# Rotary embedding on one core: whole-row stores and loads replaced by alternating two-position pieces

## The chip, the cores and the metric

The kernel runs on one core of one Trainium2 chip. The metric is the device time of one execution in microseconds (us), as the median of several runs. The core has its compute engines (TensorE, VectorE, ScalarE, GpSimd; DVE in the profile is VectorE, ACT is ScalarE, POOL is GpSimd), SyncE (SP), which issues transfers, and 16 DMA engines that move all data between main memory (HBM) and the on-chip memory (SBUF, 128 partitions).

## What is computed

The reference rotates pairs of neighbouring elements by an angle that depends on the position in the sequence. The sizes are 8 batch rows, 2048 positions, 16 heads, 64 elements per head; everything is fp32.

```python
x1 = x_pairs[..., 0]
x2 = x_pairs[..., 1]
out1 = x1 * cos - x2 * sin
out2 = x1 * sin + x2 * cos
out = np.stack([out1, out2], axis=-1).reshape(batch, seq_len, num_heads, head_dim)
```

The input and the output have 67.1 MB each, so the kernel reads and writes 134 MB of main memory; the tables have 0.26 MB each.

## The kernel before

**Tiling.** The 2048 positions of a batch row are split into 128 partitions of 16 consecutive positions (`K = 16`). In main memory the 16 positions of one partition lie together, 64 KB of fp32. On the chip a batch row is one tile of bf16, `[128, 16, 1024]`, 32 KB per partition. Loads turn fp32 into bf16 and stores turn bf16 into fp32 on the way; both are DMAs issued by GpSimd, on one queue (q0 in the profile), which the DMA engines work off in order.

**Compute.** VectorE rotates four positions at a time (`KP = 4`) with three instructions: the tile times the sine table into `qt` (line 74), the tile times the cosine table in place (line 75), and the sum of the tile and `qt` with the two elements of each pair swapped (line 80). Before that it builds the bf16 tables: `s_tab` with alternating signs (lines 94 and 95) and `c_tab` with each value twice (line 96).

**Order of the work.** The order on each engine is the order of the program text (`manual_schedule`); only the waits are placed by the framework. SP loads the first two positions of batch row 0 in fp32 (`head`, line 85, two DMAs), then the cosine table (line 86) and the sine table (line 87). GpSimd issues the load of the rest of row 0 and of rows 1 to 4, so five tiles are asked for at once (`NX = 5`, line 56). ScalarE turns the head into bf16 (line 92). Then, for each batch row, VectorE rotates it, GpSimd stores the whole row (line 59), and from the second row on GpSimd loads a further row into the tile that the row before has left; that load waits until the store of that earlier row has landed. So rows 5, 6 and 7 are loaded between the stores.

**The tail.** Of the last row GpSimd stores twelve positions. The last four (`TAIL = 4`) are turned to fp32 by ScalarE (line 117) into the buffer that the head had used and stored by SP (line 118). A one-element ScalarE copy (line 116) ahead of it writes into the tile of row 6, so it waits for that row's store.

A DMA of 128 partitions is spread over the 16 DMA engines, eight partitions to each; the trace's packet records show one packet for each partition and contiguous run.

Of the kernel before, what the change touches and what calls it, by code (L numbers as in the profile page):

```python
# [2 lines left out]

# [4 lines left out]


@with_exitstack  # L10
def kernel(
    ctx: ExitStack,
    tc: tile.TileContext,
    x: bass.AP,
    cos: bass.AP,
    sin: bass.AP,
    out: bass.AP,
):
    nc = tc.nc
    fp32 = mybir.dt.float32  # L20
    bf16 = mybir.dt.bfloat16
    mult = mybir.AluOpType.mult
    add = mybir.AluOpType.add

    B, S, H, D = x.shape
    P = 128
    K = S // P
    KP = 4
    D2 = D // 2
    HD = H * D  # L30
    NX = 5
    HEAD = 2
    TAIL = 4


    x_t = x.rearrange("b (p k) h d -> b p k (h d)", p=P, k=K)
    out_t = out.rearrange("b (p k) h d -> b p k (h d)", p=P, k=K)
    cos_t = cos.rearrange("(p k) c -> p (k c)", p=P, k=K)
    sin_t = sin.rearrange("(p k) c -> p (k c)", p=P, k=K)

    consts = ctx.enter_context(tc.tile_pool(name="consts", bufs=1))
    xpool = ctx.enter_context(tc.tile_pool(name="xpool", bufs=NX))
    qpool = ctx.enter_context(tc.tile_pool(name="qpool", bufs=1))
    stage = ctx.enter_context(tc.tile_pool(name="stage", bufs=1))

    cos_sb = consts.tile([P, K * D2], fp32)
    sin_sb = consts.tile([P, K * D2], fp32)
    c_tab = consts.tile([P, K, D], bf16)
    s_tab = consts.tile([P, K, D], bf16)

    tiles = {}

    def load(b, k0=0):
        if b not in tiles:
            tiles[b] = xpool.tile([P, K, HD], bf16, name="xt")
        nc.gpsimd.dma_start(out=tiles[b][:, k0:], in_=x_t[b, :, k0:])  # L56

    def store(b, k1=K):
        nc.gpsimd.dma_start(out=out_t[b, :, :k1], in_=tiles[b][:, :k1])  # L59

    def rotate(b, k0, k1):
        nk = k1 - k0
        xp = tiles[b][:, k0:k1]
        qt = qpool.tile([P, KP, HD], bf16, name="qt")

        def rows(a):
            return a.rearrange("p k (h e) -> p k h e", h=H, e=D)

        def tab(a):
            return dataclasses.replace(  # L70
                a, offset=a.offset + k0 * D, ap=[a.ap[0], [D, nk], [0, H], [1, D]]
            )

        nc.vector.tensor_tensor(out=rows(qt[:, :nk]), in0=rows(xp), in1=tab(s_tab), op=mult)  # L74
        nc.vector.tensor_tensor(out=rows(xp), in0=rows(xp), in1=tab(c_tab), op=mult)  # L75
        q_swap = dataclasses.replace(
            qt, offset=qt.offset + 1, ap=[qt.ap[0], [2, nk * HD // 2], [-1, 2]]
        )
        x3 = xp.rearrange("p k (a j) -> p (k a) j", j=2)
        nc.vector.tensor_tensor(out=x3, in0=x3, in1=q_swap, op=add)  # L80

    with tc.manual_schedule():
        head = stage.tile([P, TAIL, HD], fp32, name="st")
        for k in range(HEAD):
            nc.sync.dma_start(out=head[:, k : k + 1], in_=x_t[0, :, k : k + 1])  # L85
        nc.sync.dma_start(out=cos_sb, in_=cos_t)
        nc.sync.dma_start(out=sin_sb, in_=sin_t)
        load(0, HEAD)
        for b in range(1, NX):
            load(b)  # L90

        nc.scalar.copy(out=tiles[0][:, :HEAD], in_=head[:, :HEAD])  # L92
        s2 = s_tab.rearrange("p k (i j) -> p (k i) j", j=2)
        nc.vector.tensor_copy(out=s2[:, :, 0], in_=sin_sb)  # L94
        nc.vector.tensor_scalar_mul(s2[:, :, 1], sin_sb, -1.0)  # L95
        nc.vector.tensor_copy(  # L96
            out=c_tab.rearrange("p k (i j) -> p (k i) j", j=2),
            in_=cos_sb.to_broadcast([P, K * D2, 2]),
        )
        for b in range(B):  # L100
            if b == 0:
                rotate(b, 0, HEAD)
                rotate(b, HEAD, KP)
            for k0 in range(KP if b == 0 else 0, K, KP):
                rotate(b, k0, k0 + KP)
            if b < B - 1:
                store(b)

            if b >= 1 and b - 1 + NX < B:
                load(b - 1 + NX)  # L110
        store(B - 1, K - TAIL)

        tail = stage.tile([P, TAIL, HD], fp32, name="st")
        nc.scalar.copy(out=tiles[B - 2][:1, 0, :1], in_=tiles[B - 1][:1, K - 1, :1])  # L116
        nc.scalar.copy(out=tail, in_=tiles[B - 1][:, K - TAIL :])  # L117
        nc.sync.dma_start(out=out_t[B - 1, :, K - TAIL :], in_=tail)


# [1 line left out]
_INS = ['x', 'cos', 'sin']  # L122
_OUTS = [((8, 2048, 16, 64), 'float32')]


# [23 lines left out]
```

## Time and profile before

| | |
|---|---|
| median of 3 runs | 317.44 us (317.4 to 317.5) |
| span of the profiled execution | 316.0 us |
| VectorE busy | 221.8 us, 102 instructions |
| ScalarE busy | 6.9 us |
| GpSimd busy | 8.9 us |
| one VectorE instruction on four positions | 2.29 us |
| issue of one DMA on GpSimd | 0.53 to 0.67 us |
| first VectorE instruction, start of the last | at 44.2 us, at 267.1 us |

The span is the time from the first to the last instruction in one execution that the hardware profiler recorded. The page divides it into 40 equal slices; a digit is the busy share of that slice in tenths. The row named DMA is the mean share of the 16 DMA engines, and the row GB/s is what they moved, counted at the destination: a load counts with its bf16 bytes and a store with its fp32 bytes. The part on queues gives for each the packets, the megabytes and the share of the engines' time. The waits name an engine and a line, what it waited for, and then the microseconds in total, how often, and the longest.

### The profile page before, as it was taken

How to read it: one execution, taken by the hardware profiler on the slowest of the kernel's cores; microseconds unless marked ns; L12 is line 12 of the kernel's file. 1: busy time of each engine (PE TensorE's matmuls, PEld its weight loads, DVE VectorE, ACT ScalarE, POOL GpSimd, SP SyncE). 2: the span in 40 equal slices, each digit the busy share in tenths (PEclk: the TensorE clock that was granted, in tenths of full speed). 3: DMA queues.
4: the chain of work that ended last, by engine and by line, in shares of the span. 5: the costliest groups of instructions: out<-in, count | busy, mean ns of one | idle time of the engine just before them, and what ended most of it. 6: DMA issues, size and time to landing. Idle time of an engine off the chain costs nothing.

```text
span 316.0 us, 198 instructions
## 1 busy us (share of the span) xinstructions
DVE 221.8 (70%) x102; ACT 6.9 (2%) x4; POOL 8.9 (3%) x20
## 2 busy tenths in 40 slices
DVE  0000039999999999999999999999999999100000
ACT  1200000000000000000000000000000000000400
POOL 3000000000000000000000000000000000000000
DMA  9899999999999999999999999999999999999996
GB/s 241 198 257 212 212 207 236 228 199 199 253 212 265 398 498 431 398 332 261 203 399 465 328 203 199 481 448 265 199 307 423 398 440 481 406 398 481 417 431 263
DMA packets 3025, 101.72 MB, mean 322 GB/s; under 512 B 336, under 2 KB 336, under 8 KB 848
## 3 DMA queue, kind: packets, MB, share of 16 engines
q0 software_dynamic: 2304, 98.04, 96.8%
q1 hardware_dynamic: 720, 3.67, 3.1%
q14 instruction: 1, 0.01, 0.0%
HBM read 67.63 MB, written 67.11 MB: 426 GB/s over the span
## 4 chain that ended last, share of the span: by engine, by line
another core or an unknown queue 91%; DMA 2%; ACTq 1%; ACT 1%; SPq 0%; issue 0%
DMA st<-in_x_dram 2%; ACTq L144 1%; ACT xt L92 1%; ACT L92 0%; SPq L85 0%; ACT xt L116 0%; ACTq L116 0%; ACTq L92 0%
## 5 line engine op out<-in xcount | busy, mean ns | idle before, releaser
L75 DVE TENSOR_TENSOR xt<-xt,c_tab 128x4096 bf16<-128x4096 bf16 (+1 forms) x33 | 73.5, 2228 | 1.1
L80 DVE TENSOR_TENSOR xt<-xt,qt 128x4096 bf16<-128x4096 bf16 (+1 forms) x33 | 73.5, 2228 | 1.1
L74 DVE TENSOR_TENSOR qt<-xt,s_tab 128x4096 bf16<-128x4096 bf16 (+1 forms) x33 | 73.5, 2228 | 1.1
L94 DVE CAST s_tab<-sin_sb 128x512 bf16<-128x512 f32 x1 | 0.5, 453 | 44.2 <-DMA sin_sb<-in_sin_dram 44.2
L59 POOL DMA_DIRECT2D out_dram<-xt x8 | 4.3, 535 | 202.1 <-DVE xt L80 202.1
L116 ACT COPY xt<-xt 1x1 bf16<-1x1 bf16 x1 | 0.2, 193 | 286.3 <-DMA out_dram<-xt 286.3
L56 POOL DMA_DIRECT2D xt<-in_x_dram x8 | 4.4, 561 | 52.1 <-DMA out_dram<-xt 51.3
L117 ACT CAST st<-xt 128x4096 f32<-128x4096 bf16 x1 | 3.6, 3599 | 0.0
L92 ACT CAST xt<-st 128x2048 bf16<-128x2048 f32 x1 | 1.9, 1899 | 0.0
L92 ACT ACT_TABLE_LOAD x1 | 1.3, 1283 | 6.4 <-DMA st<-in_x_dram 6.4
L96 DVE CAST c_tab<-cos_sb 128x1024 bf16<-128x1024 f32 x1 | 0.7, 684 | 0.0
L95 DVE TENSOR_SCALAR s_tab<-sin_sb 128x512 bf16<-128x512 f32 x1 | 0.4, 443 | 0.0
L133 POOL MEMSET const-float32-0.0<- 128x1 f32 x1 | 0.1, 99 | 0.2 <-issue 0.2
L133 POOL MEMSET const-bfloat16-1.0<- 128x1 bf16 x1 | 0.1, 102 | 0.0
L133 POOL MEMSET const-float32-1.0<- 128x1 f32 x1 | 0.1, 99 | 0.0
L133 POOL MEMSET const-uint8-127<- 128x1 uint8 x1 | 0.1, 99 | 0.0
## 6 DMA issues: line engine op xcount, KB each, us to landing
xt<-in_x_dram POOLq DMA_DIRECT2D x7, 4096.0 KB, 58.0
out_dram<-xt POOLq DMA_DIRECT2D x1, 6144.0 KB, 49.4
xt<-in_x_dram POOLq DMA_DIRECT2D x1, 3584.0 KB, 22.7
out_dram<-st SPq DMA_DIRECT2D x1, 2048.0 KB, 15.5
st<-in_x_dram SPq DMA_DIRECT2D x2, 512.0 KB, 4.5
cos_sb<-in_cos_dram SPq DMA_DIRECT2D x1, 256.0 KB, 22.4
sin_sb<-in_sin_dram SPq DMA_DIRECT2D x1, 256.0 KB, 42.1
out_dram<-xt POOLq DMA_DIRECT2D x7, 54.0
```

The source lines that it names most:

```text
L56: nc.gpsimd.dma_start(out=tiles[b][:, k0:], in_=x_t[b, :, k0:])
L59: nc.gpsimd.dma_start(out=out_t[b, :, :k1], in_=tiles[b][:, :k1])
L74: nc.vector.tensor_tensor(out=rows(qt[:, :nk]), in0=rows(xp), in1=tab(s_tab), op=mult)
L75: nc.vector.tensor_tensor(out=rows(xp), in0=rows(xp), in1=tab(c_tab), op=mult)
L80: nc.vector.tensor_tensor(out=x3, in0=x3, in1=q_swap, op=add)
L92: nc.scalar.copy(out=tiles[0][:, :HEAD], in_=head[:, :HEAD])
L94: nc.vector.tensor_copy(out=s2[:, :, 0], in_=sin_sb)
L95: nc.vector.tensor_scalar_mul(s2[:, :, 1], sin_sb, -1.0)
L96: nc.vector.tensor_copy(out=c_tab.rearrange("p k (i j) -> p (k i) j", j=2), in_=cos_sb.to_broadcast([P, K * D2, 2]),)
L117: nc.scalar.copy(out=tail, in_=tiles[B - 1][:, K - TAIL :])
L133: nc = _bacc.Bacc("TRN2", target_bir_lowering=False, num_devices=1)
L144: with _tile.TileContext(nc) as tc:
```

## The change

From batch row 2 on, loads come in pieces of two positions (`CH = 2`, 8 KB of fp32 per partition). After each of rows 0 to 5 is rotated, GpSimd issues eight pairs in turn: the store of two positions of row b and the load of the same two positions of row b + 2 (`LEAD = 2`). Rows 0 and 1 are loaded as before, and rows 6 and 7 are each stored by one DMA; the fp32 tail with its ScalarE copies and its SP store is gone. There are four fixed tiles instead of a pool of five, and row b uses tile b mod 4. SP loads the sine table first, then the cosine table, then the head in one DMA. The VectorE instructions and their order are the same.

```diff
-    NX = 5
+    NX = 4
+    LEAD = 2
     HEAD = 2
-    TAIL = 4
+    CH = 2
...
+    head = consts.tile([P, HEAD, HD], fp32)
+    qt = consts.tile([P, KP, HD], bf16)
+    xb = [consts.tile([P, K, HD], bf16, name=f"xt{i}") for i in range(NX)]
...
+    def load(b, k0, k1):
+        nc.gpsimd.dma_start(out=xb[b % NX][:, k0:k1], in_=x_t[b, :, k0:k1])
...
+    def store(b, k0, k1):
+        nc.gpsimd.dma_start(out=out_t[b, :, k0:k1], in_=xb[b % NX][:, k0:k1])
...
-        for k in range(HEAD):
-            nc.sync.dma_start(out=head[:, k : k + 1], in_=x_t[0, :, k : k + 1])
+        nc.sync.dma_start(out=sin_sb, in_=sin_t)
         nc.sync.dma_start(out=cos_sb, in_=cos_t)
-        nc.sync.dma_start(out=sin_sb, in_=sin_t)
-        load(0, HEAD)
-        for b in range(1, NX):
-            load(b)
+        nc.sync.dma_start(out=head, in_=x_t[0, :, :HEAD])
+        load(0, HEAD, K)
+        for b in range(1, LEAD):
+            load(b, 0, K)
...
-            if b < B - 1:
-                store(b)
-
-            if b >= 1 and b - 1 + NX < B:
-                load(b - 1 + NX)
-        store(B - 1, K - TAIL)
-
-
-
-        tail = stage.tile([P, TAIL, HD], fp32, name="st")
-        nc.scalar.copy(out=tiles[B - 2][:1, 0, :1], in_=tiles[B - 1][:1, K - 1, :1])
-        nc.scalar.copy(out=tail, in_=tiles[B - 1][:, K - TAIL :])
-        nc.sync.dma_start(out=out_t[B - 1, :, K - TAIL :], in_=tail)
+            if b + LEAD < B:
+                for k0 in range(0, K, CH):
+                    store(b, k0, k0 + CH)
+                    load(b + LEAD, k0, k0 + CH)
+            else:
+                store(b, 0, K)
```

## The prediction

> **What bounds the kernel now.** I read the page first, its busy shares and its rows of slices, then the waits, then a table of stretches, and last the DMA packet records in the trace, which the page only sums.
>
> ```profile
> DVE 221.8 (70%) x102; ACT 6.9 (2%) x4; POOL 8.9 (3%) x20
> ...
> DMA  9899999999999999999999999999999999999996
> GB/s 241 198 257 212 212 207 236 228 199 199 253 212 265 398 498 431 398 332 261 203 399 465 328 203 199 481 448 265 199 307 423 398 440 481 406 398 481 417 431 263
> ...
> q0 software_dynamic: 2304, 98.04, 96.8%
> q1 hardware_dynamic: 720, 3.67, 3.1%
> ...
> HBM read 67.63 MB, written 67.11 MB: 426 GB/s over the span
> ```
>
> The DMA row is 9 in nearly every slice: the 16 DMA engines are the bound, and no other engine is near it. The two queues together fill 99.9% of the span. The GB/s row counts bytes at the destination, so a stretch of loads (fp32 read, bf16 written) shows about 200 and a stretch of stores (bf16 read, fp32 written) over 400, at the same load of the engines. The waits say who stands behind the DMA:
>
> ```profile
> POOL out_dram L59 <- DVE xt L80: 202.1, 8, 70.5
> POOL xt L56 <- DMA out_dram<-xt: 51.3, 3, 21.7
> DVE s_tab L94 <- DMA sin_sb<-in_sin_dram: 44.2, 1, 44.2
> ```
>
> DVE starts only at 44.2 us, because the sine table comes in between load packets. GpSimd waits 202.1 us for DVE. Neither empties the DMA queue, which the next table shows: stretches cut so that each holds one whole store or load (store, store, load, store, load; the columns are busy times, granted TensorE clock, DMA share, GB/s).
>
> ```profile
> 101.79:121.10 19.31, 19.00 (x10) 0.00 (x0) 0.54 (x1) 1.00 1.02 434
> 121.10:140.42 19.32, 19.05 (x9) 0.00 (x0) 1.07 (x2) 1.00 1.02 410
> 140.42:159.74 19.32, 19.05 (x9) 0.00 (x0) 1.07 (x2) 1.00 1.00 238
> 159.74:179.05 19.31, 19.00 (x10) 0.00 (x0) 0.00 (x0) 1.00 1.02 412
> 179.05:198.37 19.32, 19.05 (x9) 0.00 (x0) 1.07 (x2) 1.00 1.01 239
> ```
>
> A store and a load of one batch row each take 19.3 us, whatever stands before or after them. So the time is a sum over what each DMA engine carries, one packet after the other, and the change must be priced in packets.
>
> **The packet rows.** All of these are starts of consecutive packets on one engine, from the trace's packet records. A batch row is eight packets per engine, one for each partition that it serves. A load packet of 65,536 bytes read starts 2,413 ns after the one before, a store packet of 65,536 bytes written 2,412 ns. The last store, cut to twelve positions, has packets of 49,152 bytes at 1,809.4 ns. The two store rows give (2,411.75 - 1,809.4) / 16,384 = 36.77 ps per byte, and leave 2,411.75 - 65,536 x 0.03677 = about **2.3 ns per store packet** that is not bytes. For loads the shorter form is 57,344 bytes at 2,203.5 ns, with one table packet between each two; that packet costs 2,504.6 - 2,412.9 = 91.7 ns in the next load, so 2,111.8 ns without it, 301.1 ns per 8,192 bytes, and **about 4 ns per load packet** is left. Where one DMA ends and the next begins on the queue, the first step is longer: 2,452 ns after a store (and the next one shorter, 2,393), 2,434 after a load (then 2,412). Net of the shorter step that is **about 21 ns per DMA boundary**, after a store and after a load alike.
>
> **The change, part by part.**
>
> *Pieces of two positions.* Loads of rows 2 to 7 and stores of rows 0 to 5 become 96 DMAs of eight packets per engine; a packet is 8,192 bytes on its wide side instead of 65,536. The bytes are the same. Each piece has eight packets per engine where the same bytes were one before, so seven more: 48 store pieces x 7 x 2.3 ns = 0.8 us, 48 load pieces x 7 x 4 ns = 1.3 us. Together **+2.1 us**, all on the path, since the engines have no idle time to hide it.
>
> *More DMAs.* The GpSimd queue had 16 and gets 2 + 96 + 2 = 100. 84 more boundaries x 21 ns = **+1.8 us**, on the path for the same reason. [...]
>
> *Does it run dry?* The compiled order shows that completion semaphores go round in eight, so from then on each GpSimd DMA waits for the one eight places before it. Behind a waiting DMA stand all later stores and loads, and DVE waits for those loads. Up to seven DMAs are then still queued, 7 x 2.45 = 17 us of work, against an issue of 0.53 to 0.55 us (rows of L56 and L59). At the start: loads 0 and 1 keep the engines busy until about 43 us (load 0 lands at 23.9 us now, load 1 is 19.3 us more). The tables are now first, so DVE can start when the head is in, at some 8 to 12 us, and goes on with row 0 at 24 us; four positions take three instructions of 2.29 us, 6.98 us in steps. By 43 us some ten positions of row 0 are done and seven pieces (17 us) stand in the queue; row 0 is done at about 24 + 14/4 x 6.98 = 48.4 us. After that one row of store and load takes DMA 39.5 us and DVE 27.9 us, so DVE is ahead, then idles for loads, and each store is ready long before its turn: a piece of row b+2 lands one whole turn of 39.5 us before its store is due, and DVE needs 7 us of it. Had the tables not moved, DVE would start at 44.2 us as now, and the queue would run empty for some 5 to 10 us. [...]
>
> *Tables first, one head DMA, no tail in fp32, four buffers.* The head and tables are the same bytes on the same engines: nothing. DVE starting earlier buys nothing by itself, since DVE is not the bound. The tail was eight SP packets of 16,384 bytes at 607 ns, 4.86 us, and becomes two packets more of the last store, 4.82 us: nothing. The ScalarE cast of 3.6 us lay beside twelve positions of the last store. Four buffers instead of five are enough, since load b+2 fills the buffer that store b-2 left a turn earlier.
>
> *The sum.* 316.0 (span) + 2.1 + 1.8 = 319.9 us. Around the span lie 317.44 - 316.0 = 1.4 us of the median, which I keep: **321.3 us**. The median of three runs is 317.44 (317.4 to 317.5), and the profile's span stands 0.5% under it. Bounds: below, 2.3 ns for every packet (1.5 us) and 9 ns per boundary (the shortest duration of the 4-byte packet that ends a DMA; 0.8 us), 319.7 us. Above, 4.4 ns per packet (the 4,096-byte head packets step by 155 ns, of which 150.6 are bytes; 3.0 us), 40 ns per boundary (3.4 us) and one more us for the spread of the engines' ends (1.6 us at the last round now), 324.8 us. I take the middle, because it comes from the same queue and kinds of packet.
>
> **The rivals.**
>
> *Reads and writes overlap (faster).* A load keeps an engine's read side full and its write side half full, a store the other way round. Side by side a pair would need 98,304 bytes each way, 3.61 us instead of 4.82: 1.2 us x 48 pairs = 58 us off, 263 us; DVE (24 + 219.7 us of work) and a last store of 19.3 us set a floor at about 265 us. [...] Against it: in the trace a load that follows a store starts 2,452 ns after it, exactly as a store that follows a store does, and takes its full 2,431 ns. If an engine read ahead across such a boundary, one of the two would be shorter. And the alternation is no finer than that: a piece is eight packets, 65,536 wide bytes per engine, the same amount between two turns as one packet of now. It outweighs the added costs from 3.9 us / 48 = 81 ns of overlap per pair; the trace shows none.
>
> *GpSimd's issue becomes the bound (much slower).* One DMA must leave GpSimd every 2.46 us. [...] If a DMA took g us, the price is 96 x (g - 2.46): 13 us at 2.6, so 335 us; it decides from g = 2.46, 4.5 times the row.
>
> *No difference.* The small costs hide, for example because packets of one DMA run closer together than two DMAs do: 317.4 to 318.
>
> **How the numbers follow.** Forecast of serial packets, 319.7 to 324.8: 0.80. Overlap, 265 to 316: 0.09. Issue or a dry queue, over 326: 0.07. No difference: 0.04. A measurement of this kernel can tell about 0.2% from no change. Faster 0.09, same 0.04, slower 0.80 + 0.07 = 0.87. The range goes a little beyond the forecast's bounds on both sides, 318.5 to 326, and leaves the overlap and the dry queue out.
>
> **What would show it.** Right: the DMA row stays at 9 to the end; the GB/s row becomes even, near 320, in the middle; packets step by 303 to 306 ns; 100 GpSimd DMAs of about 0.54 us each (54 us busy); DVE starts near 4 us with the tables and waits for loads from row 4 on. Overlap: the GB/s row goes clearly above 330 in the middle and DVE's share goes towards 84%. Issue bound: DMA slices of 7 or 8, and GpSimd waiting for nothing. A dry queue at the start: a DMA slice under 9 near 43 us.

## The result and the profile after

| | before | after |
|---|---|---|
| median | 317.42 us (317.39 to 317.50, 4 runs) | 327.60 us (326.82 to 327.74, 4 runs) |
| ratio, 95% interval | | 1.0313 (1.0301 to 1.0325) |
| span of the profiled execution | 316.0 us | 325.1 us (that run: 326.82 us) |

The change makes the kernel 10.2 us slower. The sign is the one forecast; the size is not: 3.9 us were forecast, and 327.6 us lies above the range of 318.5 to 326. One execution in what follows, 330.85 us of the whole rows with the tables first, was in a slower state of the chip and is left out of that run's figures.

The page of the changed kernel, the rows that were read of the kernel before:

```profile
DVE 222.0 (68%) x102; ACT 3.2 (1%) x2; POOL 53.5 (16%) x104
...
DMA  7999989999999999999999999999999999999990
GB/s 167 261 255 201 238 247 324 326 310 327 324 312 327 322 311 331 319 314 330 317 314 332 314 319 329 315 320 329 311 324 326 313 323 326 449 387 476 427 387 40
...
q0 software_dynamic: 14400, 100.15, 102.8%
q1 hardware_dynamic: 432, 1.57, 1.3%
...
HBM read 67.63 MB, written 67.11 MB: 415 GB/s over the span
```

The middle is as forecast: the DMA row stays at 9, and the GB/s row is even at 310 to 332, because each slice now holds as many loads as stores. Two things are new. The first slice is a 7 where it was a 9, and the last slice is a 0 where it was a 6: for some 5 us at the end, no DMA engine moves anything (the DMA share from 320.18 us to the end is 0.00). The waits on GpSimd:

```profile
POOL out_dram L55 <- DVE xt L75: 80.0, 7, 35.5
POOL out_dram L55 <- DMA out_dram<-xt: 75.4, 36, 2.2
POOL xt L52 <- DMA xt<-in_x_dram: 70.6, 41, 1.9
```

The 36 and 41 short waits, of at most 2.2 us, are those on the DMA eight places earlier on GpSimd's queue. They empty nothing, since seven more DMAs stand in the queue, of 2.4 to 2.5 us each. The same stretches as before the change, which held a store or a load of 19.3 us each:

```profile
101.79:121.10 19.31, 19.04 (x9) 0.00 (x0) 4.26 (x8) 1.00 1.09 322
121.10:140.42 19.32, 19.05 (x9) 0.00 (x0) 4.25 (x8) 1.00 1.09 321
140.42:159.74 19.32, 19.05 (x9) 0.00 (x0) 4.26 (x8) 1.00 1.09 321
```

Each now holds both kinds (322, 321, 321 GB/s). The DMA share of 1.09 is no overlap of reads and writes: a packet of 8,192 bytes lasts 322 to 341 ns by its record, while the next starts after some 304, and the share adds the durations.

**Where the time is, in the middle.** Each DMA ends with a 4-byte packet on every engine: q0 has 256 of them before for 16 DMAs, and 1,600 after for 100. Their mean over the 16 engines gives the step from one DMA to the next. Before, a store and a load of a row took 19,295 + 19,343 = 38,638 ns. After, a store piece and a load piece take 2,438 + 2,469 = 4,907 ns, and eight such pairs 39,256. So a row costs 618 ns more, and six rows 3.7 us.

**Where it is, at the end.** SP waits for all DMAs, then for the other engines. SP's waits in the kernel before and in the changed one:

```profile
SPq L144 <- PEq L144: 0.6, 2, 0.4
```

```profile
SPq L130 <- DMA out_dram<-xt: 48.4, 1, 48.4
SPq L130 <- PEq L130: 4.4, 2, 4.0
```

The page names PEq, but it is the barrier at the end of the program, and the one engine that is late to it is GpSimd. Its last instruction before the barrier is a DRAIN, which starts at 288.83 us, as GpSimd issues its last DMA (288.85 us). In the instruction records the last data land at 320.18 us (a landing is the moment at which a DMA has reported on all 16 engines that it is done), the DRAIN ends at 324.31, and the span ends at 325.06: 4.88 us behind the last landing. The 4.13 us from GpSimd's last landing to the end of its DRAIN are called the drain lag below. Before, the DRAIN ended at 312.79 us, while SP's tail was still being stored (last landing 315.14), and 0.87 us of span were left. So **4.0 us more lie behind the last byte**, in an instruction that no group of the page shows.

**Where it is, at the start.** By the records of the 4-byte packets, five of the 16 engines end load 0 1.3 to 1.5 us later than the mean; before, the latest was 0.5 us late. They stay behind to the last store, where the latest is 1.6 us late. The packet records show where this begins: GpSimd's first packet starts at 3.3 to 4.3 us on eleven engines and at 5.4 to 5.7 us on five. The records do not name the engine, so it is by their number that these five are taken for the same.

### The profile page after: what moved, and what is told of

It reads as the page before. It is cut to its first block, busy times and chain, and to the rows that moved or that the text cites. A ratio compares the mean times of both kernels' runs of the same rounds, so it can differ in the third digit from the quotient of the medians.

```text
span 325.1 us, 308 instructions
## 1 busy us (share of the span) xinstructions
DVE 222.0 (68%) x102; ACT 3.2 (1%) x2; POOL 53.5 (16%) x104
## 3 DMA queue, kind: packets, MB, share of 16 engines
q0 software_dynamic: 14400, 100.15, 102.8%
## 4 chain that ended last, share of the span: by engine, by line
DMA 80%; DVE 4%; issue 3%; ACT 1%; POOL 0%; SPq 0%; POOLq 0%
DMA xt<-in_x_dram 70%; DMA head<-in_x_dram 9%; DVE qt L69 1%; DVE xt L75 1%; DVE xt L70 1%; ACT xt L85 1%; POOL out_dram L55 0%; POOLq L130 0%; POOL xt L52 0%; SPq L79 0%; SPq L78 0%; POOLq L55 0%
## 5 line engine op out<-in xcount | busy, mean ns | idle before, releaser
L55 POOL DMA_DIRECT2D out_dram<-xt x50 | 26.9, 537 | 164.2 <-DVE xt L75 80.0
L52 POOL DMA_DIRECT2D xt<-in_x_dram x50 | 26.6, 533 | 71.4 <-DMA xt<-in_x_dram 70.6
L85 ACT CAST xt<-head 128x2048 bf16<-128x2048 f32 x1 | 1.9, 1897 | 29.7 <-DMA head<-in_x_dram 29.7
## 6 DMA issues: line engine op xcount, KB each, us to landing
xt<-in_x_dram POOLq DMA_DIRECT2D x48, 512.0 KB, 19.3
```

The source lines that it names most:

```text
L52: nc.gpsimd.dma_start(out=xb[b % NX][:, k0:k1], in_=x_t[b, :, k0:k1])
L55: nc.gpsimd.dma_start(out=out_t[b, :, k0:k1], in_=xb[b % NX][:, k0:k1])
L85: nc.scalar.copy(out=xb[0][:, :HEAD], in_=head[:, :HEAD])
```

## The experiments

The ratio is that to the kernel before, measured on the same chip (317.43 to 317.51 us there), with its 95% interval.

### Is it the missing tail? The kernel before without it

```diff
-            if b < B - 1:
-                store(b)
+            store(b)
...
-        store(B - 1, K - TAIL)
...
-        tail = stage.tile([P, TAIL, HD], fp32, name="st")
-        nc.scalar.copy(out=tiles[B - 2][:1, 0, :1], in_=tiles[B - 1][:1, K - 1, :1])
-        nc.scalar.copy(out=tail, in_=tiles[B - 1][:, K - TAIL :])
-        nc.sync.dma_start(out=out_t[B - 1, :, K - TAIL :], in_=tail)
```

> The kernel before, but the last row is stored whole by GpSimd (17 -> 16 queue DMAs stay 16), with no fp32 tail on SP. In the changed kernel GpSimd's closing drain ends 4.1 us after the last data have landed; in the kernel before 0.7 us. Theory A (the drain grows with the number of GpSimd DMAs, about 0.04 us each): 16 DMAs, drain 0.7 us after the last landing, time 317 to 318 us. Theory B (whenever the last store is GpSimd's, the drain costs some 4 us, and the SP tail only covered it): 320.5 to 321.5 us. The prediction had costed the tail at nothing, as theory A does.

Measured: 317.99 us (317.80 to 318.19), ratio 1.0014 (1.0006 to 1.0023). SP's wait at the barrier:

```profile
SPq L135 <- PEq L135: 0.9, 2, 0.5
```

The drain ends 0.70 us after the last landing. Theory B falls: a GpSimd store at the end does not by itself cost 4 us. The tail alone was worth about half a microsecond: without it 1.43 us of the span lie behind the last landing instead of 0.87.

### Half as many pieces

```diff
-    CH = 2
+    CH = 4
```

> The changed kernel with pieces of four positions: 52 GpSimd DMAs instead of 100, packets of 16,384 bytes. Packet and boundary costs by the prediction's rows: 24 pairs x (6 x 2.3 + 6 x 4) ns = 0.9 us and 36 more boundaries than before x 21 ns = 0.8 us, so 1.7 us instead of 3.9. Theory A: the drain lag falls from 4.1 to about 2.1 us, so in all some 4 us less than the changed kernel, 323 to 324 us. Theory B: the lag stays at 4, only 2.2 us less, 325 to 326 us.

Measured: 322.36 us (321.05 to 324.43), ratio 1.0161 (1.0132 to 1.0190).

```profile
SPq L130 <- PEq L130: 2.4, 2, 2.0
```

The drain lag is 2.17 us; the line through 16 DMAs (0.70) and 100 (4.13) gives 2.17 for 52. A pair of pieces takes 9,726 ns. With the pair of two positions (4,907) that is two equations: if the part that is not bytes is the same for both, a pair is its bytes (4,819 ns for 131,072 bytes) plus 88 ns. The time is a little below the 323 to 324 us of theory A, but the runs differ by 3.4 us among themselves, so it is the lag that tells the theories apart. In the profiled one a single engine is 2.6 us late at load 0 and 3.2 us late at the end, and the span ends with that engine.

### The head first

```diff
+        nc.sync.dma_start(out=head, in_=x_t[0, :, :HEAD])
         nc.sync.dma_start(out=sin_sb, in_=sin_t)
         nc.sync.dma_start(out=cos_sb, in_=cos_t)
-        nc.sync.dma_start(out=head, in_=x_t[0, :, :HEAD])
```

> The changed kernel, with SP loading the head first, then the sine and the cosine table. In the changed kernel the head's 8 KB packets come in between load 0's packets and land at 31.7 us, the engines idle 0.75 us more than before in the first 10 us, and they end 1.6 us apart from their mean instead of 0.7. If the order of SP's loads makes that: head at 6 to 8 us, engine ends as in the kernel before, 1 to 2 us less than the changed kernel, 325.5 to 326.5 us. If the spread comes from the pieces: same time as the changed kernel within 0.5 us. The drain lag stays at about 4 us under both theories A and B.

Measured: 325.67 us (325.64 to 325.75), ratio 1.0258 (1.0245 to 1.0271): 1.9 us less than the changed kernel, and steady (this is the head-first kernel of the later runs). All engines end load 0 within 0.7 us of their mean. The waits for the head and the tables, first in the changed kernel, then here:

```profile
ACT xt L85 <- DMA head<-in_x_dram: 29.7, 1, 29.7
...
DVE c_tab L89 <- DMA cos_sb<-in_cos_dram: 7.2, 1, 7.2
...
DVE s_tab L87 <- DMA sin_sb<-in_sin_dram: 3.5, 1, 3.5
```

```profile
DVE c_tab L89 <- DMA cos_sb<-in_cos_dram: 18.3, 1, 18.3
DVE s_tab L87 <- DMA sin_sb<-in_sin_dram: 14.4, 1, 14.4
ACT xt L85 <- DMA head<-in_x_dram: 3.3, 1, 3.3
```

What SP asks for last came in between the packets of GpSimd's loads: the head landed at 31.7 us in the changed kernel, eight of its packets on each engine among the load's, and the cosine table at 33.5 us here. VectorE starts on row 0 at 33.7 and 34.1 us, so the order buys it nothing. The drain lag is 4.13 us, as with the tables first.

### The same pieces, not alternating

```diff
                 for k0 in range(0, K, CH):
                     store(b, k0, k0 + CH)
+                for k0 in range(0, K, CH):
                     load(b + LEAD, k0, k0 + CH)
```

> The changed kernel with the same 96 pieces, but all eight stores of a row first and then its eight loads, so that a store follows a store and a load a load. If reads and writes do not overlap at the turn from store to load (the prediction's forecast), the step of a piece stays and the time is that of the changed kernel within 0.5 us. If the alternation gains something that the extra costs hide, this one is slower, by 48 x the overlap per pair: 2 us or more for 40 ns.

Measured: 327.13 us (325.33 to 327.95), ratio 1.0293 (1.0268 to 1.0318). The GB/s row of its page shows that stores and loads now come in blocks:

```profile
GB/s 178 283 233 196 254 288 427 375 211 217 377 433 346 214 210 422 428 310 215 243 427 423 277 212 281 422 434 232 217 310 433 407 220 211 440 387 491 411 387 24
```

A store piece steps by 2,449 ns and a load piece by 2,458, together 4,907 ns, the very step of the alternating pair. Here alternation neither gains nor costs. The rival of overlapping reads and writes is out, at this grain of 65,536 wide bytes per engine between two turns.

### Pieces of one position

```diff
-    CH = 2
+    CH = 1
```

> The changed kernel with pieces of one position: 196 GpSimd DMAs, packets of 4,096 bytes on the wide side. From the steps measured so far (4,907 ns for a pair of two positions, 9,726 for a pair of four) a pair costs its bytes plus 88 ns whatever its size, so a pair of one position should step by 2,498 ns. 96 such pairs take 239.8 us, 4.2 us more than 48 of two positions. Theory A (the closing drain ends 0.70 us + 0.0408 us per DMA above 16 after the last landing; it fits 16, 52 and 100 DMAs): 8.04 us, 3.9 us more than the changed kernel. Together about 335.7 us, within 1.5 us for the start. Theory A': the drain's lag has a ceiling or depends on the bytes: lag 4 to 5 us, 332 us.

Measured: 330.13 us (329.09 to 331.65), ratio 1.0402 (1.0370 to 1.0434). A pair takes 1,243 + 1,255 = 2,498 ns, as worked out. But the drain lag is 3.72 us and not 8.04: the straight line of theory A falls, and the time is below the 332 us of theory A' too. In GpSimd's waits and SP's there is a trace of why:

```profile
POOL xt L52 <- issue: 3.3, 1, 3.3
```

```profile
SPq L130 <- PEq L130: 4.0, 2, 3.5
```

Once, GpSimd stands still for 3.3 us without waiting for anything that the profile shows: in front of its 114th DMA. The line gives 3.72 us for 90 DMAs, 196 - 106. So the new theory (R) was that GpSimd does at this stop what the closing drain would have had to do for 106 DMAs, and that the drain pays for what is left. What it does there, and why at the 114th, the trace does not show.

### The tail kept, beside 100 DMAs

The head-first kernel, with the tail of the kernel before:

```diff
-            else:
+            elif b < B - 1:
                 store(b, 0, K)
+        TAIL = 4
+        store(B - 1, 0, K - TAIL)
+        tail = consts.tile([P, TAIL, HD], fp32)
+        nc.scalar.copy(out=xb[(B - 2) % NX][:1, 0, :1], in_=xb[(B - 1) % NX][:1, K - 1, :1])
+        nc.scalar.copy(out=tail, in_=xb[(B - 1) % NX][:, K - TAIL :])
+        nc.sync.dma_start(out=out_t[B - 1, :, K - TAIL :], in_=tail)
```

> The changed kernel with the head first and with the fp32 tail of the kernel before kept (the last four positions turned to fp32 by ScalarE and stored by SP): 100 GpSimd DMAs as before. In the kernel before, GpSimd's last data land 3.0 us ahead of SP's. If the closing drain runs from GpSimd's own last landing, its 4.1 us begin 3.0 us earlier and only about 1.1 us of it stands behind the last byte: about 322.7 us, 3.0 us less than the same kernel without the tail (325.67). If the drain waits for all DMAs, SP's too: no gain, 325.5 to 326 us.

Measured: 322.84 us (322.49 to 322.95), ratio 1.0165 (1.0151 to 1.0179), 2.8 us less than without the tail. The drain ends 1.10 us after the last landing of all.

```profile
SPq L136 <- DMA out_dram<-tail: 2.8, 1, 2.8
SPq L136 <- PEq L136: 1.6, 2, 1.2
```

The drain runs from GpSimd's own last landing (its lag is 4.13 us here too), and SP's store, which lands 3.0 us later, covers that much of it. The line above has 2.8 us of this as SP's wait. That is what the tail of the kernel before hides, besides its own transfer.

### One head DMA in the kernel before

```diff
-        for k in range(HEAD):
-            nc.sync.dma_start(out=head[:, k : k + 1], in_=x_t[0, :, k : k + 1])
+        nc.sync.dma_start(out=head[:, :HEAD], in_=x_t[0, :, :HEAD])
```

> The kernel before with its head loaded by one DMA (packets of 8,192 bytes instead of two DMAs with packets of 4,096), the only part of the change that could have gained: with the head as one DMA in first place, the engines idled 0.4 us between 2 and 6 us, and 1.05 us in the kernel before. If that is the start's cost, 0.4 to 0.7 us less than the kernel before: 316.8 to 317.1 us. If the engines' late start is set by GpSimd's first load anyway (its first packet at 5.1 us in both): 317.3 to 317.6 us.

Measured: 317.85 us (317.41 to 318.38), ratio 1.0013 (1.0004 to 1.0022). A miss: the fuller start is no gain. The engines' mean end is where it was (the store of row 6 ends at 294.82 us on the mean, 294.66 before), and the latest engine is 1.15 us late there instead of 0.72. No version here beats the kernel before.

### Whole rows, with the tables first and with the head first

Two runs take away the pieces alone and keep the rest of the change, with three rows loaded ahead so that the queue holds work for longer. The second also puts the head first.

```diff
-    LEAD = 2
+    LEAD = 3
-    CH = 2
+    CH = 16
```

> The changed kernel with whole rows (16 GpSimd DMAs): four fixed buffers, sine table first, one head DMA, no tail, and three rows loaded ahead, so that the queue holds work until row 0 is rotated. It takes away the pieces alone. By the parts found so far: the drain lag 0.7 us, no cost of pieces, and the start's cost of SP's order (some engines up to 2.5 us behind from the first load on, different from run to run) stays: 318 to 320 us with a spread between runs of 1 us or more. If the pieces alone made all of the loss: 317.5 to 318.2 us.

> Whole rows (16 GpSimd DMAs, three rows loaded ahead, four fixed buffers, no tail) with the head first, in one DMA. Against the whole rows with the tables first (320.55 us) it moves only SP's order. If the order makes the start's loss, this is as the kernel before without its tail (317.99 us): 317.8 to 318.4 us. If fixed buffers or the three rows ahead cost something themselves: 319 us or more.

Measured: with the tables first 320.2 us, the median of four executions of 319.6 to 320.7 us (the 320.55 us of the second expectation is that of all five), ratio 1.0084 (1.0071 to 1.0098); with the head first 319.52 us (319.35 to 319.59), ratio 1.0065 (1.0053 to 1.0078). The drain lag is 0.70 us in both. With the tables first the time is just above the expected 318 to 320 us, and not at 317.5 to 318.2, so the pieces did not make all of the loss. With the head first the runs are steady again, but 1.5 us above the kernel without a tail, a miss of 1.1 us against the expectation. The steps name it: the first store, after load 2, takes 21,524 ns instead of 19,324, since the queue ran empty for 2.2 us. It is the 6 in the eighth slice:

```profile
DMA  9899999699999999999999999999999999999996
```

VectorE had started at 34 us and row 0 was not done; its store was issued at 63.0 us, after load 2 had ended. That is the dry queue that the prediction had priced; whole rows have no early piece to store. The 2.2 us are the mean of the engines. The wait also brought them together (the latest was 0.68 us behind the mean before it and 0.10 after it), so the latest one lost 1.6 us. That covers the 1.5 us, and the fixed buffers and the order of the rows show no cost beside it.

### Is it the head's late packets? No head at all

```diff
-    head = consts.tile([P, HEAD, HD], fp32)
...
-        nc.sync.dma_start(out=head, in_=x_t[0, :, :HEAD])
-        load(0, HEAD, K)
+        load(0, 0, K)
...
-        nc.scalar.copy(out=xb[0][:, :HEAD], in_=head[:, :HEAD])
```

> The changed kernel (tables first, pieces of two positions) without the separate head: row 0 is loaded whole by GpSimd, so that SP carries only the two tables. In the runs with the tables first some engines end load 0 a whole load packet (2.1 to 2.4 us) behind the rest and stay there, and the time differs by 1 to 3 us from run to run; with the head first this is gone. Theory S1 (it comes from the head's packets, still waiting when GpSimd's first load starts): without them the engines stay together and the time is steady, 325 to 326 us. Theory S2 (it comes from the tables being first, so that GpSimd's first packets start on some engines at 3.4 us and on others at 5.6): the spread stays, 326 to 328 us with 1 us or more between runs. VectorE starts row 0 at about 24 us in both, early enough for the queue.

Measured: 327.14 us (325.73 to 327.49), ratio 1.0297 (1.0278 to 1.0317). The spread stays: three engines end load 0 0.9 to 1.4 us late, and load 1 1.5 to 1.9 us. Theory S1 falls: the head's packets are not needed for it.

### More DMAs, a shorter drain

The head-first kernel with rows 6 and 7 stored in pieces too:

```diff
             else:
-                store(b, 0, K)
+                step = CH if b < B - 1 else 1
+                for k0 in range(0, K, step):
+                    store(b, k0, k0 + step)
```

> The head-first kernel with pieces (325.67 us), with row 6 stored in eight pieces of two positions and row 7 in sixteen of one: 122 GpSimd DMAs instead of 100. With 196 DMAs the closing drain was 3.7 us, not the 8.0 of the straight line, and GpSimd stood 3.28 us still in front of its 114th DMA. Theory R (GpSimd cleans up after its DMAs once its list is full, at the 114th, and the closing drain pays only for what is left; 196 - 106 = 90 fits 3.72 us): the drain lag is 0.5 to 1.0 us, the stall at the 114th is hidden by the seven DMAs in the queue, and the time falls: 22 more boundaries x 44 ns = 1.0 us more, 3.3 us less drain, 323.0 to 323.8 us. Theory A'' (the drain grows to about 4 us and stays there): 326.5 to 327 us.

Measured: 323.03 us (322.91 to 324.39), ratio 1.0189 (1.0172 to 1.0206): 22 DMAs more, and 2.6 us less. The timeline of GpSimd around its 114th DMA (start, duration, what, and in brackets the idle time before it), and SP's wait:

```profile
297.75 0.53 POOL L55 DMA_DIRECT2D out_dram<-xt  x1 [1.90 <-DMA out_dram<-xt]
302.77 2.12 POOL L55 DMA_DIRECT2D out_dram<-xt  x4 [4.49 <-issue]
305.17 0.53 POOL L55 DMA_DIRECT2D out_dram<-xt  x1 [0.28 <-DMA out_dram<-xt]
```

```profile
SPq L132 <- PEq L132: 1.1, 2, 0.6
```

GpSimd stands still for 4.49 us, then issues four DMAs in a row that had become free meanwhile. The queue has work for that long: in that stretch row 6's pieces still step by 2,449 to 2,450 ns and row 7's, of one position, by 1,244 to 1,245, so it costs nothing. The drain lag is 0.696 us, that of 16 DMAs, and 122 - 106 = 16. Theory R was made from the run with 196 DMAs and forecast this one's lag and time rightly. What GpSimd does while it stands still, no record shows, nor that a list is full there: that part of the theory was the author's guess.

### The order of SP's loads, in the kernel before

```diff
-        for k in range(HEAD):
-            nc.sync.dma_start(out=head[:, k : k + 1], in_=x_t[0, :, k : k + 1])
-        nc.sync.dma_start(out=cos_sb, in_=cos_t)
         nc.sync.dma_start(out=sin_sb, in_=sin_t)
+        nc.sync.dma_start(out=cos_sb, in_=cos_t)
+        nc.sync.dma_start(out=head[:, :HEAD], in_=x_t[0, :, :HEAD])
```

> The kernel before with nothing changed but SP's order: sine table, cosine table, then the head in one DMA. The same order cost 1.9 us in the kernel with pieces (327.60 against 325.67 us with the head first), and without a head the engines still ended load 0 up to 1.4 us behind their mean. If the order alone makes that loss (theory S2), it does so here too: 318.8 to 320 us, with 1 us or more between runs and some engines 1 us or more behind the mean from load 0 on. If it only costs together with pieces or with the earlier start of VectorE's stores: 317.3 to 318 us and steady.

Measured: 319.34 us (318.80 to 319.52), ratio 1.0055 (1.0041 to 1.0069). Three engines end load 0 1.1 to 1.5 us late and the store of row 6 1.5 to 1.9 us late. The tables first, with the head in one DMA behind them, cost 1.8 us, with no piece anywhere. The edit also makes one DMA of the head's two, which in first place was 0.36 us slower (317.85 against 317.49), so about 1.5 us are left for the order itself. The executions differ by 0.7 us, less than the 1 us expected. The wait for the sine table falls from 44.2 us to 3.5, and nothing is gained by it:

```profile
DVE s_tab L93 <- DMA sin_sb<-in_sin_dram: 3.5, 1, 3.5
```

## Why the prediction was wrong, point by point

The 10.2 us are made up of: pieces 3.7 (steps of the DMAs), closing drain 4.0 (behind the last byte), order of SP's loads 1.9 (327.60 against 325.67). That is 9.6, and 0.6 us are left. One head DMA instead of two, 0.36 us in the kernel before, may be part of it; the rest stays open. The first two figures are from the two profiled executions, whose spans differ by 9.05 us; the third is a difference of medians.

- **What bounds the kernel**: right. The DMA engines carry packets one after the other (store and load pieces step by 2,438 and 2,469 ns, the pair by 4,907 in either order), and the middle is their sum.
- **Pieces and boundaries, +3.9 us**: right for the queue, 3.7 us measured. The split was 37 to 49 ns for a DMA of eight small packets; three sizes give 44 (half of the 88 of a pair). What the step lacks is that each of the 84 DMAs costs a second time, at the end: 84 x 40.8 ns = 3.4 us of closing drain.
- **The queue does not run dry**: right for the change. The first stores were issued at 38 us, ahead of the end of load 1 at 44. The starting time of VectorE was wrong, though: row 0 began at 33.7 us and not at 8 to 12, because the head, last in SP's order, landed at 31.7. That the conclusion held was in part luck: there was little in hand, and it held only because two positions can be stored as soon as they are rotated; with whole rows and the same start, 2.2 us were lost.
- **"Tables first, one head DMA, ...: nothing"**: wrong, by 1.9 us in the changed kernel and 1.5 to 1.8 in the kernel before. The step counted bytes. The bytes are the same, but in the changed kernel five engines end load 0 1.3 to 1.5 us behind the mean, no later step let them catch up (the same five, by their number, are 1.3 to 1.6 us behind at the last store), and the end waits for the last one. The four buffers show no cost (whole rows with the head first).
- **"No tail in fp32: nothing"**: the step that failed most. It compared the transfer of the tail with that of two more packets, which was right (without the tail the last landing is at 314.96 us instead of 315.14), and never asked what SP's store, landing last, hid: GpSimd's closing drain. With 16 DMAs the tail is worth half a microsecond, with 100 it is worth 2.8. So of the 4.0 us behind the last byte, 0.56 come with the tail's end alone (0.87 to 1.43 us at 16 DMAs), and the other 3.4 are the drain's growth with 84 more DMAs.
- **"Around the span lie 1.4 us, which I keep"**: wrong in kind. What stands behind the last byte is inside the span, and it went from 0.87 to 4.88 us. The 1.4 was also too small: executions of 317.4 to 317.5 us have spans of 315.7, so the outside is about 1.75 us, and the profiled execution was 0.3 us slower than the median.
- **The rivals**: the overlap is out (4,907 ns in both orders), and that an engine reads for one packet while it writes for another was an assumption that no run shows; the issue on GpSimd never bound, 0.53 to 0.67 us for each DMA. The 0.07 for over 326 us stood for a slow issue or a dry queue, and neither came. None of the rivals was the closing drain, and the range, made from packet rows alone, could not hold it.

In what would have shown it, the prediction looked at the middle, and there its signs came true: 320 GB/s, 53.5 us of issue, VectorE's first instruction at 3.5 us. Its one sign for the end, a DMA row at 9, did not. The row that it lacked was in the trace of before: GpSimd's DRAIN ended 0.7 us after its own last landing, with 16 DMAs.

## What to carry to other kernels

In this kernel, with its DMA engines full, cutting transfers cost 44 ns for each DMA in the queue, which could be read from the steps, and alternating the kinds gave nothing back (4,907 ns a pair in both orders). Such a sum is about the middle only: ask what the last instruction of each engine has to do after the last byte (here 4.13 us of drain), and which transfer hides it (here the tail, 2.8 us). A change of order at the start that moves no byte can still leave some engines behind: here 1.3 to 1.5 us after load 0 and still up to 1.6 us at the end. Where the queue ran empty for 2.2 us (whole rows with the head first), the wait brought them together, from 0.68 us behind the mean to 0.10.

## What the runs showed of the hardware

- **GpSimd's closing drain grew with its DMAs.** It ended after GpSimd's last landing by 0.696 us with 16 DMAs, 2.166 with 52 and 4.125 with 100: 0.043 us + 40.8 ns for each. In front of the 114th DMA GpSimd stands still once (3.28 us in the run with 196 DMAs, 4.49 us in that with 122), and from there on the lag is that of 106 DMAs fewer: 0.696 us with 122 and 3.718 with 196. All these DMAs have eight packets of data and one of 4 bytes on each engine (q0 has 2,304 packets for 16 DMAs, 14,400 for 100, 28,224 for 196), so whether the price is for a DMA or for its packets was not told apart.
- **A queued DMA of eight packets per engine cost 44 ns beyond its bytes**, at 4, 8 and 16 KB packets alike (pairs of 2,498, 4,907 and 9,726 ns, 88 ns of each not bytes). These are steps from one DMA to the next with the next one already in the queue.
- **Which engines fall behind at the start** differed between the runs. With the tables first, one, three, five or seven of them end load 0 from 0.8 to 2.6 us behind the mean; with the head first the latest is 0.5 to 0.9 us behind. With the tables first, GpSimd's first packets appear at 3.3 to 4.3 us on most engines and at up to 6.1 on others; with the head first, at 5.1 to 6.0 on all. In the trace with one late engine one first packet is late (5.6 us, the others 3.4 to 3.8), and with seven seven are (4.8 to 6.1, the others 3.6 to 3.9). Why the first packet is late on them was not settled.
